# Moving the first LayerNorm's gain and offset off the router's path in a one-core decoder layer

## The chip, the cores and the metric

One core of one Trainium2 chip runs the whole layer in one launch. The metric is device time in microseconds (us). The kernel before took 1308.48 to 1312.22 us in three runs, median 1310.56 us.

## The reference, cut to what matters

256 tokens of width 1024 go through a token mixer (a Mamba-2 scan and sliding-window attention off one projection), a first LayerNorm, and a mixture of 32 experts of which each token takes four; then the second LayerNorm.

```python
m = token_mixer(x, ...)                       # 256 x 1024
h = layer_norm(alpha * x + m, ln1_g, ln1_b)   # alpha = 2 ** 0.25
logits = h @ w_router + b_router              # 1024 x 32, top 4, softmax over the four
y = layer_norm(alpha * h + moe(h), ln2_g, ln2_b)
# expert: hgu = h @ w_gate_up[e] + b; act = clamped SwiGLU; act @ w_down[e] + b_down[e]
```

All is float32. The experts' weights are 32 x (8 MB + 4 MB), read once each.

## The kernel before, in words

The order of the instructions is written out by hand, and every engine runs its own list in that order. There are three stretches.

**The front** (lines 197 to 832) multiplies x by the combined projection in slices of 256 columns. Each slice is a 1 MB load into one of two ring buffers (SP's queue, L110), is split by ACT into a rounded high part and by DVE into the remainder (L67 and L70, `split_ahead`), and costs 2 x 24 products on TensorE (PE, `mm3`). A count called `clock` goes up after each 24 products (`tick`), and side work is put on that count with `later(d, fn)`: convolution taps on DVE, the decays of the scan, attention heads. `part_dt` (L712) so sets `decays` (a small product, whose result ACT copies to `acn`) at count DD = 6 and `decay_rows` (L513, a PE transpose of `acn`, stored to DRAM) at DD + 1. The loads for the later norm and router are issued by `mix_loads` (L694) during the gate slices: x again, the rows of `ln1_g` and `ln1_b` spread over 128 partitions (512 KB each), the router's weights and bias. After the projection come the attention output product (the loop at L787, four slices), the scan's output product (L815) and the merge.

**The router stage** (L835 to L975) runs the mixing product in eight pieces `mix(c, q)` of 12 products each, for two halves c of the tokens and four weight pieces q. After a column half is complete, `resid` adds alpha * x on DVE and takes norm statistics. Then, per token half: `first_norm` (mean and reciprocal deviation by a logarithm, an exponential and a Newton step, then four DVE passes with gain and offset), `turn` (eight PE transposes of h, copied by ACT to `hT`), `logits` (eight products), `residual` (alpha * h into the four output banks by a product with `ia`), `top` (bias, top four as a mask `mk`), `place` (each token's position in its expert's list by a product with a triangular matrix) and `one_hot`. `gather(None, 0)` (L1209) then builds the inputs of experts 0 and 1 by products of h with the one-hot matrix, one ACT copy per four blocks.

**The experts** (L1215 to L1241) run a list of 384 steps ("slots"): eight steps u per expert for gate and up, four steps d for down, those of expert e - 1 after the u of expert e. A 2 MB weight tile feeds two steps. The tiles are loaded by SP (L140) into ten buffers (`NPAIR`); nine are asked for ahead, seven from expert 25 on (`st["ahead"]`); a load waits until PE has finished with the tile that held its buffer. In the router stage `prefetch(n)` issues the first ten as buffers come free. `at(n, fn, pre)` hangs further work on step n, ahead of (pre) or behind its products. Every second expert brings a gather of 16 products; every expert a transposed gate matrix S and the product `out` that adds its rows to the four output banks `po`, which stay taken from the router stage to the end. After the u steps of expert 27 all engines branch over a block for overfull experts (`overflow`, L1205), which these inputs never enter. Behind the last step the rows of `ln2_g` and `ln2_b` are loaded, spread over the partitions, and the second norm runs on DVE straight from the output banks.

Of the kernel before, what the change touches and what calls it, by code (L numbers as in the profile page):

```python
# [8 lines left out]
F = mybir.dt.float32  # L9
R = mybir.dt.float32r  # L10
I32 = mybir.dt.int32
AF = mybir.ActivationFunctionType
# [3 lines left out]
P = 128  # L16
# [6 lines left out]
NE = 32  # L23
# [21 lines left out]
def hybrid_layer(ctx, tc, x, w_in, conv_w, conv_b, dt_bias, a_log, d_skip, norm_w, w_ssm_out,  # L45
# [201 lines left out]
    for _ in range(2):  # L247
# [32 lines left out]
    io64 = const.tile([P, 2, 64], F, name="io64")  # L280
    nc.gpsimd.iota(io64, pattern=[[0, 2], [1, 64]], base=0, channel_multiplier=0,
                   allow_small_or_imprecise_dtypes=True)
# [358 lines left out]
    def rstd(dst, var, n, scale, eps, tag):  # L641

        v, y, t = [work.tile([P, n], F, name=x_ + tag, tag=x_, bufs=2) for x_ in ("rs_v", "rs_y", "rs_t")]
        ts(v, var, scale, eps, OP.mult, OP.add)
        act(y, v, AF.Ln)
        act(y, y, AF.Exp, scale=-0.5)

        def newton():
            tt(t, y, y, OP.mult)
            tt(t, t, v, OP.mult)  # L650
            ts(t, t, -0.5, 1.5, OP.mult, OP.add)
            tt(dst, y, t, OP.mult)
        return newton
# [4 lines left out]
    def gated():  # L658
# [33 lines left out]
        prefetch(1)  # L692

    def mix_loads():  # L694
        xr = single.rearrange("p (c d) -> p c d", d=D)
        nc.sync.dma_start(xr, x[0].rearrange("(c p) d -> p c d", p=P))
        lnc = [w4([P, D], n) for n in ("lng", "lnb")]
# [3 lines left out]
        nc.sync.dma_start(wr3, w_router[0].rearrange("(k p) e -> p k e", p=P))  # L701
        br = w1([P, 32], "br")
        nc.sync.dma_start(br, rows(b_router, 32))
        return xr, lnc, wr3, br

    mixin = []


# [75 lines left out]
    for i in range(2):  # L784
        nc.sync.dma_start(bgn[i], b_gate_up[0, :, D * i:D * i + D])
    mrg = gts[1]
    for n in range(4):  # L787
        hi, lo = take()
        for b in range(2):
# [48 lines left out]

    def mix(c, q):
# [5 lines left out]
        for k in range(4):  # L845
# [5 lines left out]
    xr, lnc, wr3, br = mixin  # L851
    bst = work.tile([P, 2, 2, 6], F, name="bst", bufs=1)
# [6 lines left out]
    hn = xr  # L859
    hT = [None, None]  # L860
# [4 lines left out]
    ones = const.tile([P, P], F, name="ones")  # L865
    lg, mk = (const.tile([P, 2, 32], F, name=n) for n in ("lg", "mk"))
# [3 lines left out]
    ts(ia, ident, ALPHA, None, OP.mult)  # L870
    nc.vector.memset(ones, 1.0)

# [11 lines left out]

    def norm(dst, src, bs, gb, tag):

        mean, r = norm_scale(bs, tag)()
        for hf in range(2):
            hs = slice(512 * hf, 512 * hf + 512)
            norm_half(dst[:, hs], src[hf], mean, r, gb, hs)  # L890

    def turn(c):
        hT[c] = w4([P, 8, P], f"hT{c}")
        for k4 in range(2):
            pb = bank(f"ht{c}{k4}").rearrange("p (k t) -> p k t", k=4)
            for k in range(4):
                nc.tensor.transpose(pb[:, k], hn[:, c, (4 * k4 + k) * P:(4 * k4 + k + 1) * P], ident)
            act(hT[c][:, 4 * k4:4 * k4 + 4], pb)

    pl = [None, None]  # L900

    def logits(c):
        pl[c] = bank(f"lg{c}")[:, 0:32]
        for k in range(8):
            mm(pl[c], hT[c][:, k], wr3[:, k], k == 0, k == 7)

    def top(c):
        tt(lg[:, c], pl[c], br, OP.add)
        nc.vector.max(t8[:, c], lg[:, c])
        ts(nm[:, c:c + 1], t8[:, c, 0:1], -1.0, None, OP.mult)  # L910
        nc.vector.memset(t8[:, c, 4:8], 3.0e38)
        nc.vector.match_replace(rp[:, c], t8[:, c], lg[:, c], -3.0e38)
        ts(mk[:, c], rp[:, c], -2.9e38, None, OP.is_le)

    pp = bank("pos").rearrange("p (c e) -> p c e", e=32)
    G2 = const.tile([P, 2, 2, 64], F, name="G2")

    def place(c):
        mm(pp[:, c], slt, mk[:, c], c == 0, True)
        stt(posm[:, c], pp[:, c], 1.0, mk[:, c], OP.add, OP.mult)  # L920
        ts(posm[:, c], posm[:, c], -1.0, None, OP.add)

# [8 lines left out]

    def residual(c):
        for hf in range(2):
            po[c][hf] = bank(f"out{c}{hf}")
            hs = slice(512 * hf, 512 * hf + 512)
            mm(po[c][hf], ia, hn[:, c, hs], True, False)

    def first_norm(c):
        norm(hn[:, c], [xr[:, c, 0:512], xr[:, c, 512:1024]], bst[:, c].rearrange("p a b -> p (a b)"), lnc, f"l1{c}")

# [34 lines left out]
    one_hot(0, 1)  # L975
    nxt_moe = nxt[0]
    assert nxt_moe == S_E
# [45 lines left out]
    def gather(n, j):  # L1023

        if n is not None:
            one_hot(j, 0)
            one_hot(j, 1)
        XG[j] = more.tile([P, 2, 8, 64], F, name=f"xg{j}", tag="xg")

        def unit(kq, n):  # L1030
            pb = bank(f"xg{j}{kq}").rearrange("p (q n) -> p q n", q=4)
            for k in range(4):
                o = 256 * (2 * kq + k // 2) + k % 2
                for c in range(2):
                    mm(pb[:, k], hn[:, c, o:o + 255:2], G2[:, c], c == 0, c == 1)
            ev = lambda: act(XG[j][:, :, 4 * kq:4 * kq + 4].rearrange("p e q s -> p q e s"),
                             pb.rearrange("p q (e s) -> p q e s", e=2))
# [69 lines left out]
    def done_d(n, e, b_, S):  # L1107
        y = mo.tile([P, 512], F, name="y", bufs=2)
        last = e == NE - 1

        def f():
            for c in range(2):
                for hf in range(2):
                    rs = slice(64 * hf, 64 * hf + 64)
                    mm(po[c][hf], S[rs, c * P:(c + 1) * P], y[rs], False, last)
        if last:
            act(y, b_)
            f()
        else:
            at(n + 1, lambda: act(y, b_))  # L1120
            at(n + 1, f, pre=False)


    def overflow():
        ns = (NT - cap) // 2

        def half(t, *shape):
# [11 lines left out]
        Ss = half(mo.tile([P, 512], F, name="y", bufs=2), 2, NT)  # L1139
        nc.gpsimd.iota(ios, pattern=[[ns, 2], [1, ns]], base=cap, channel_multiplier=0,  # L1140
                       allow_small_or_imprecise_dtypes=True)

        def big(w, c0, lhs, e):
            for kp in range(4):
# [3 lines left out]
                else:  # L1148
                    rows_ = w[0, e, 256 * kp:256 * (kp + 1), c0:c0 + 1024].rearrange("(k p) n -> p k n", p=P)
                nc.gpsimd.dma_start(raw, rows_)  # L1150
# [20 lines left out]
        def one_expert(e):  # L1171
            for s in range(2):
# [3 lines left out]
                for k4 in range(2):  # L1176
                    pb = bk[k4][:, 0:4 * ns].rearrange("p (k n) -> p k n", n=ns)
                    for k in range(4):
                        kk = slice((4 * k4 + k) * P, (4 * k4 + k + 1) * P)
                        for c in range(2):  # L1180
                            mm(pb[:, k], hn[:, c, kk], gs[:, 0, c], c == 0, c == 1)
                    act(xg[:, s, 4 * k4:4 * k4 + 4], pb)
                for c in range(2):
# [21 lines left out]
        with tc.If(cv > cap):  # L1205
            for e in range(NE):
                one_expert(e)

    gather(None, 0)  # L1209
    at(0, lambda: (soft(0), soft(1), nc.scalar.preload_act_table_set(SILU)), pre=False)  # L1210
# [32 lines left out]

    lnd, res = (t.rearrange("p (s d) -> p s d", d=D) for t in pair("lnd"))
    lnd = [lnd[:, 0], lnd[:, 1]]
    nc.sync.dma_start(lnd[0], rows(ln2_g, D))
    nc.sync.dma_start(lnd[1], rows(ln2_b, D))
    work = mo
# [42 lines left out]
```

## Time and profile before

| what | value |
|---|---|
| median of the runs, us | 1310.56 |
| profiled execution, us | 1311.2 |
| its span, us | 1309.4 |
| PE busy, share of span | 95% |
| PE weight loads busy | 51% |
| DVE, ACT busy | 32%, 23% |
| HBM read | 465.30 MB, 356 GB/s over the span |
| SP's queue (q1), share of 16 DMA engines | 85.7% |

The profiled execution took 1311.2 us, of which 1309.4 us are the span that the trace shows and 1.8 us lie around it. The trace names engines PE, PEld (PE's weight loads), DVE, ACT, POOL and SP. A time in a row is the start from the beginning of the span; what stands in square brackets is the idle time before an instruction on its engine, and what ended it. Matmul ends are modelled, so PE's spare time is read from bracketed idle times and from the distances between starts, not from its busy share. A float32 product is recorded as two matmuls.

### The profile page before, as it was taken

The page shows a single profiled execution, that of the slowest core. Times are in us where ns is not written, and L with a number is a line of the kernel's source. Part 1 is how long each engine was busy: PE and PEld are TensorE (multiplying, and loading weights), DVE is VectorE, ACT ScalarE, POOL GpSimd, SP SyncE. Part 2 cuts the span into 40 slices and gives each one's busy share as a digit, 9 for nine tenths or more (in the row PEclk, how much of TensorE's full clock was granted, in tenths as well). Part 3 has the DMA queues.
Part 4 walks back from the last instruction along what each step waited for, and adds up shares of the span by engine and source line. Part 5 has one row for each costly group of instructions (what it writes and reads, how often), then busy time and mean ns, then how long its engine had stood idle before and what let it go on. Part 6 is the DMA issues. An engine that isn't in the chain of part 4 may idle for free. (4 is left out here: it accounts for less than half of the span.)

```text
span 1309.4 us, 16114 instructions
## 1 busy us (share of the span) xinstructions
PE 1237.4 (95%) x6835; PEld 673.5 (51%) x6835; DVE 421.5 (32%) x813; ACT 300.0 (23%) x535; POOL 23.7 (2%) x28
## 2 busy tenths in 40 slices
PE   8899999999999999999999989899998989879995
PEld 7898878999974343343443424333333424323331
DVE  4889986665651211121111111111111111111114
ACT  3657676634411010111100101010010101000001
POOL 0001210000000000000000000000000000000000
PEclk9899999999989999999999999999999999989998
DMA  6444445776699999999999999999999999999994
GB/s 214 152 159 133 158 161 162 242 277 245 226 410 384 430 429 431 430 429 431 430 430 430 431 432 428 430 430 431 431 430 430 430 430 430 432 426 430 430 431 175
DMA packets 80003, 467.50 MB, mean 357 GB/s; under 512 B 7052, under 2 KB 46164, under 8 KB 55220
## 3 DMA queue, kind: packets, MB, share of 16 engines
q1 hardware_dynamic: 78500, 460.99, 85.7%
q0 software_dynamic: 1200, 4.33, 1.0%
q8 instruction: 55, 0.90, 0.2%
q10 hardware_dynamic: 224, 1.08, 0.2%
q14 instruction: 24, 0.20, 0.0%
HBM read 465.30 MB, written 1.08 MB: 356 GB/s over the span
## 5 line engine op out<-in xcount | busy, mean ns | idle before, releaser
L81 PE MATMUL u<-w,xg 128*64 128x512 f32 x2048 | 462.2, 597 | 19.7 <-DMA w<-in_w_gate_up_dram 19.6
L81 PEld LDWEIGHTS u<-w,xg 128*64 128x64 f32 x2048 | 140.3, 137 | 309.9 <-issue 259.3
L81 PE MATMUL d<-w,ac 128*64 128x512 f32 x1024 | 241.7, 603 | 19.1 <-DVE gg L75 9.0
L1054 DVE COPY gu<-u 128x512 f32<-128x512 f32 x32 | 22.1, 692 | 678.6 <-PE u L81 678.6
L81 PE MATMUL ws<-x,w 128*128 128x256 f32 x1200 | 156.6, 291 | 1.9 <-ACT w L67 1.8
L81 PEld LDWEIGHTS ws<-x,w 128*128 128x128 f32 x1200 | 149.8, 196 | 5.5 <-ACT w L67 2.4
L81 PEld LDWEIGHTS d<-w,ac 128*64 128x64 f32 x1024 | 68.5, 137 | 141.9 <-issue 132.8
L70 DVE TENSOR_TENSOR w<-ring,w 128x2048 fp32r<-128x2048 f32 (+1 forms) x51 | 115.4, 2268 | 38.2 <-ACT w L67 36.5
L67 ACT ACTIVATE w<-ring 128x2048 fp32r<-128x2048 f32 (+1 forms) x51 | 95.5, 1876 | 64.2 <-DMA ring<-in_w_in_dram 19.1
L67 ACT ACTIVATE gu<-u 128x512 f32<-128x512 f32 x32 | 19.1, 597 | 319.8 <-PE u L81 319.8
L81 PEld LDWEIGHTS xg<-G,single 128*128 128x128 f32 x512 | 62.9, 197 | 25.0 <-issue 24.3
L81 PE MATMUL xg<-G,single 128*128 128x128 f32 x512 | 68.9, 288 | 0.4 <-DVE G L70 0.4
L67 ACT ACTIVATE xg<-xg 128x512 f32<-128x512 f32 x32 | 19.1, 597 | 219.2 <-PE xg L81 219.2
L81 PE MATMUL out<-y,S 64*128 64x512 f32 x256 | 63.6, 615 | 0.8 <-ACT y L67 0.8
L67 ACT ACTIVATE hg<-hg 128x512 f32<-128x512 f32 x32 | 20.2, 631 | 147.8 <-DVE hg L74 147.8
L81 PE MATMUL yss<-yt,w 128*128 128x256 f32 x384 | 48.3, 289 | 0.2 <-DVE w L70 0.2
L81 PEld LDWEIGHTS yss<-yt,w 128*128 128x128 f32 x384 | 47.7, 198 | 0.6 <-DVE w L70 0.4
L81 PE MATMUL z<-w,x 128*128 128x512 f32 x192 | 47.9, 402 | 0.0
L1065 PEld LDWEIGHTS tu<-ident,gu 128*128 128x128 f32 x256 | 33.4, 210 | 25.5 <-issue 24.3
L81 PEld LDWEIGHTS out<-y,S 64*128 64x128 f32 x256 | 22.0, 186 | 41.9 <-issue 40.2
L67 ACT ACTIVATE y<-d 128x512 f32<-128x512 f32 x32 | 19.1, 597 | 105.5 <-PE d L81 105.5
L70 DVE TENSOR_TENSOR hg<-tu,bgu 128x256 f32<-128x256 f32 x64 | 26.9, 420 | 48.5 <-PE tu L1065 48.4
(214 smaller groups left out, 808.7 us busy)
## 6 DMA issues: line engine op xcount, KB each, us to landing
w<-in_w_gate_up_dram SPq DMA_DIRECT2D x128, 2048.0 KB, 38.1
w<-in_w_down_dram SPq DMA_DIRECT2D x63, 2048.0 KB, 38.7
ring<-in_w_in_dram SPq DMA_DIRECT2D x33, 1024.0 KB, 5.1
ring<-in_w_ssm_out_dram SPq DMA_DIRECT2D x8, 1024.0 KB, 5.1
E<-accd POOLq DMA_DIRECT2D x8, 512.0 KB, 4.6
ring<-in_w_attn_out_dram SPq DMA_DIRECT2D x4, 1024.0 KB, 5.2
ring<-in_w_mix_out_dram SPq DMA_DIRECT2D x4, 1024.0 KB, 7.2
single<-in_x_dram SPq DMA_DIRECT2D x2, 512.0 KB, 3.6
```

Source lines behind the costliest of these rows:

```text
L67: return nc.scalar.activation(o, i, func, **kw)
L70: return nc.vector.tensor_tensor(o, a, b, op=op)
L81: return nc.tensor.matmul(o, l, r, start=start, stop=stop)
L1054: nc.vector.tensor_copy(t, banks[hf])
L1065: nc.tensor.transpose(pb[:, b], gu[hf][:, b:b + 509:4], ident)
```

## The change

1. **Router.** The logits are formed from the residual before normalization. The gain is multiplied into the router's weights and each expert's column mean is taken off them (`router_parts`, hung on the second slice of the attention output product), so that the mean of the row drops out; the deviation is applied to the 32 logits in `top`. The offset's share goes into the bias. Transposes (`turn`) now run on the residual and are spread between the pieces of the mixing product, and `logits(0)` stands inside the last piece.
2. **Gather.** `normed` (one ACT pass) only takes off the mean and scales; gain and offset come in when the gathered rows are copied (four ACT copies in place of one). The gather of experts 0 and 1 is issued per token half.
3. **Late work.** The residual's product, and the rows of ln1 and ln2 spread over partitions by small products (`norm_rows`) from one 16 x 256 tile `lnr`, are done in steps 356 to 377 of 384, at experts 30 and 31 (and the down steps of 29 and 30).
4. **Smaller ones.** `decay_rows` two counts later; one DVE operation less in the one-column Newton step and in `place` (positions count from 1); the spread loads of the four norm vectors fall away; the never-entered overflow block follows the new gather.

```diff
+    lnr = const.tile([16, 256], F, name="lnr")
+    gbc = const.tile([P, 2, 8], F, name="gbc")
...
-        nc.sync.dma_start(lnc[0], rows(ln1_g, D))
-        nc.sync.dma_start(lnc[1], rows(ln1_b, D))
+        for i, v in enumerate((ln1_g, ln1_b, ln2_g, ln2_b)):
+            nc.sync.dma_start(lnr[4 * i:4 * i + 4], v[0].rearrange("(t n) -> t n", n=256))
...
+    def router_parts():
+        wr3 = mixin[1]
+        pb = bank("lncol")
+        for j in range(2):
+            nc.tensor.transpose(pb[:, 16 * j:16 * j + 16], lnr[:, j:j + 255:2], ident[0:16, 0:16])
+        act(gbc.rearrange("p i (t j) -> p j i t", j=2),
+            pb[:, 0:32].rearrange("p (j i t) -> p j i t", j=2, t=4)[:, :, 0:2])
...
+        def sums_():
+            tt(t, wr3, gbc[:, 1].unsqueeze(2).to_broadcast([P, 8, 32]), OP.mult)
+            nc.vector.tensor_reduce(red[:, 32:64], t.rearrange("p k e -> p e k"), op=OP.add, axis=AX.X)
+            tt(wr3, wr3, gbc[:, 0].unsqueeze(2).to_broadcast([P, 8, 32]), OP.mult)
+            nc.vector.tensor_reduce(red[:, 0:32], wr3.rearrange("p k e -> p e k"), op=OP.add, axis=AX.X)
+        def centred():
+            mm(pb[:, 64:128], ones, red, True, True)
+            stt(wr3, pb[:, None, 64:96].to_broadcast([P, 8, 32]), -1.0 / D, wr3, OP.mult, OP.add)
+            tt(br, br, pb[:, 96:128], OP.add)
+        later(1, sums_)
+        later(3, centred)
...
-        later(DD + 1, decay_rows)
+        later(DD + 3, decay_rows)
...
     for n in range(4):
         hi, lo = take()
+        if n == 1:
+            router_parts()
...
     def top(c):
-        tt(lg[:, c], pl[c], br, OP.add)
+        stt(lg[:, c], pl[c], scales[c][1], br, OP.mult, OP.add)
...
+    def normed(c):
+        mean, r = scales[c]
+        off = work.tile([P, 1], F, name="no", bufs=2)
+        stt(off, mean, -1.0, r, OP.mult, OP.mult)
+        act(xr[:, c], xr[:, c], AF.Identity, scale=r, bias=off)
...
     resid(0, 1)
+    turn(0, 0)
+    turn(1, 0)
+    first_scale(0)
     mix(1, 2)
-    first_norm(0)
-    mix(1, 3)
+    turn(0, 1)
+    scales[0] = scales[0]()
+    normed(0)
+    mix(1, 3, 0)
+    logits(0)
+    mix(1, 3, 1)
+    top(0)
     resid(1, 1)
     prefetch(10)
-    turn(0)
-    first_norm(1)
-    logits(0)
-    residual(0)
-    top(0)
-    turn(1)
     place(0)
+    turn(1, 1)
+    first_scale(1)
     one_hot(0, 0)
     logits(1)
     mm(pp[:, 1], ones, mk[:, 0], True, False)
-    residual(1)
+    scales[1] = scales[1]()
     top(1)
+    normed(1)
+    xg0 = [bank(f"xg0{kq}").rearrange("p (q n) -> p q n", q=4) for kq in range(2)]
+    first_rows(0, 0)
     place(1)
+    first_rows(0, 1)
     one_hot(0, 1)
+    first_rows(1, 0)
+    first_rows(1, 1)
...
+            def ev():
+                for k in range(4):
+                    kk = 4 * kq + k
+                    act(XG[j][:, :, kk], pb[:, k].rearrange("p (e s) -> p e s", e=2), AF.Identity,
+                        scale=gbc[:, 0, kk:kk + 1], bias=gbc[:, 1, kk:kk + 1])
...
+    def norm_rows(n, i, hf):
+        pb = bank(f"row{i}{hf}")
+        for r in range(2):
+            t = 4 * i + 2 * hf + r
+            mm(pb[:, 256 * r:256 * r + 256], ident[0:16, t:t + 1].to_broadcast([16, P]), lnr, True, True)
+        hs = slice(512 * hf, 512 * hf + 512)
+        def use():
+            if i >= 2:
+                act(lnd[i - 2][:, hs], pb)
+            else:
+                for c in range(2):
+                    tt(hn[:, c, hs], hn[:, c, hs], pb, OP.add if i else OP.mult)
+        at(n + 1, use)
+    def residual():
+        for c in range(2):
+            for hf in range(2):
+                mm(po[c][hf], ia, hn[:, c, 512 * hf:512 * hf + 512], False, False)
...
+    LATE = 8 + 12 * (NE - 3)
+    for q in range(4):
+        at(LATE + 2 * q, lambda q=q: norm_rows(LATE + 2 * q, q // 2, q % 2), pre=False)
+        at(LATE + 12 + 3 * q, lambda q=q: norm_rows(LATE + 12 + 3 * q, 2 + q // 2, q % 2), pre=False)
+    at(LATE + 10, residual, pre=False)
+    at(LATE + 11, out_tiles)
...
-    nc.sync.dma_start(lnd[0], rows(ln2_g, D))
-    nc.sync.dma_start(lnd[1], rows(ln2_b, D))
```

## Rows read from the trace of the kernel before

**Rows 1.** The page, GB/s moved in 40 equal slices of the span.
```profile
GB/s 214 152 159 133 158 161 162 242 277 245 226 410 384 430 429 431 430 429 431 430 430 430 431 432 428 430 430 431 431 430 430 430 430 430 432 426 430 430 431 175
```

**Rows 2.** Windows: stretch, length, busy time per engine, PE clock, DMA share, GB/s.
```profile
380.00:390.00 10.00, 9.57 (x44) 7.32 (x45) 1.66 (x10) 0.60 (x1) 0.50 (x1) 0.68 1.02 416
390.00:400.00 10.00, 10.00 (x53) 3.93 (x51) 1.11 (x8) 2.30 (x4) 0.00 (x0) 1.00 0.62 231
```

**Rows 3.** Timeline of SP's queue, weight tiles of the experts, router stage.
```profile
349.47 19.35 SPq L140 DMA_DIRECT2D w<-in_w_gate_up_dram  x6
...
394.58 11.34 SPq L140 DMA_DIRECT2D w<-in_w_gate_up_dram  x4
```

**Rows 4.** Timeline of PE after the expert-27 branch, up to the last expert's down steps.
```profile
1167.71 5.50 PE L81 MATMUL d<-w,ac 128*64 128x512 f32 x16 [8.63 <-DVEq L1205]
...
1264.27 3.65 PE L81 MATMUL u<-w,xg 128*64 128x512 f32 x16 [0.20 <-DMA w<-in_w_gate_up_dram]
1269.34 3.65 PE L81 MATMUL u<-w,xg 128*64 128x512 f32 x16 [1.41 <-DMA w<-in_w_gate_up_dram]
1274.28 1.94 PE L81 MATMUL d<-w,ac 128*64 128x512 f32 x8 [1.29 <-DVE gg L75]
...
1283.97 1.94 PE L81 MATMUL d<-w,ac 128*64 128x512 f32 x8 [0.77 <-DMA w<-in_w_down_dram]
```

**Rows 5.** Timeline of the front around the transpose of acn: PE, DVE, SP's queue.
```profile
53.38 0.42 PE L515 MATMUL acT<-ident,acn 128*64 128x128 f32 x1 [5.88 <-ACT acn L67]
53.45 16.95 PE L81 MATMUL ws<-x,w 128*128 128x256 f32 x120
...
57.67 6.34 SPq L110 DMA_DIRECT2D ring<-in_w_in_dram  x2
...
64.75 2.29 DVE L70 TENSOR_TENSOR w<-ring,w 128x2048 fp32r<-128x2048 f32 x1 [0.46 <-ACT w L67]
...
72.83 2.29 DVE L70 TENSOR_TENSOR w<-ring,w 128x2048 fp32r<-128x2048 f32 x1 [0.28 <-PE s L81]
```

**Rows 6.** Tile ring, loads from 20 to 120 us: issue to landing.
```profile
DMA to landing us min/median/max: 5.0/5.2/6.3
```

**Rows 7.** Windows of the front, columns as in rows 2.
```profile
50.00:60.00 10.00, 6.62 (x36) 6.63 (x37) 9.79 (x16) 5.41 (x12) 0.00 (x0) 0.66 0.55 160
150.00:160.00 10.00, 10.00 (x70) 8.94 (x69) 9.79 (x21) 9.32 (x24) 4.27 (x3) 1.00 0.33 107
290.00:300.00 10.00, 10.00 (x84) 9.82 (x82) 2.03 (x4) 2.24 (x2) 0.00 (x0) 1.00 0.83 311
```

**Rows 8.** Timeline, a small product inside the expert steps.
```profile
399.62 0.63 PE L81 MATMUL pos<-mk,ones 128*128 128x32 f32 x4
400.18 7.09 PE L81 MATMUL u<-w,xg 128*64 128x512 f32 x32
```

**Rows 9.** Timeline of PE in the router stage.
```profile
372.31 1.97 PE L81 MATMUL lg<-wr,hT 128*128 128x32 f32 x16
...
378.98 3.08 PE L81 MATMUL lg<-wr,hT 128*128 128x32 f32 x16
...
382.30 3.76 PE L81 MATMUL out<-single,ia 128*128 128x512 f32 x4
...
390.89 8.80 PE L81 MATMUL u<-w,xg 128*64 128x512 f32 x40
```

**Rows 10.** Timeline of PE around the product with the down bias.
```profile
897.95 1.94 PE L81 MATMUL d<-w,ac 128*64 128x512 f32 x8
899.82 3.69 PE L81 MATMUL out<-bd,S 32*128 32x512 f32 x8
903.45 1.94 PE L81 MATMUL d<-w,ac 128*64 128x512 f32 x8
```

**Rows 11.** Windows late in the experts, columns as in rows 2.
```profile
1182.00:1235.00 53.00, 53.00 (x260) 20.75 (x258) 8.36 (x22) 5.61 (x10) 0.00 (x0) 1.00 1.01 430
```

**Rows 12.** Lines by form: busy, mean ns | idle before, releaser.
```profile
L70 DVE TENSOR_TENSOR rs_tl<-rs_tl,rs_vl 128x1 f32<-128x1 f32 x4 | 0.6, 159 | 0.1
```

More of the change, by code (lines that the diff above doesn't have):

```diff
@@ L648, in newton @@
         def newton():
-            tt(t, y, y, OP.mult)
-            tt(t, t, v, OP.mult)
+            if n == 1:
+                stt(t, y, v, y, OP.mult, OP.mult)
+            else:
+                tt(t, y, y, OP.mult)
+                tt(t, t, v, OP.mult)
             ts(t, t, -0.5, 1.5, OP.mult, OP.add)
@@ L692, in gated @@
         prefetch(1)
+    lnr = const.tile([16, 256], F, name="lnr")
+    gbc = const.tile([P, 2, 8], F, name="gbc")
+    ones = const.tile([P, 1], F, name="ones").to_broadcast([P, P])
+    br = sm("br", 32)
     def mix_loads():
@@ L786, in hybrid_layer @@
     mrg = gts[1]
+    nc.vector.memset(ones[:, 0:1], 1.0)
     for n in range(4):
         hi, lo = take()
+        if n == 1:
+            router_parts()
         for b in range(2):
@@ L837, in hybrid_layer, with mix @@
     pm = [[bank(f"mix{c}{hf}") for hf in range(2)] for c in range(2)]
-    def mix(c, q):
+    def mix(c, q, part=None):
         hf, kh = divmod(q, 2)
@@ L844, in mix @@
         cs = slice(c * P, (c + 1) * P)
-        for k in range(4):
+        for k in range(4) if part is None else (2 * part, 2 * part + 1):
             kk = 4 * kh + k
@@ L849, in mix @@
             mm(pm[c][hf], ml[:, kk, cs], hi[:, k], False, kk == 7)
[L851 removed]
+    xr, wr3 = mixin
     bst = work.tile([P, 2, 2, 6], F, name="bst", bufs=1)
@@ L859, in hybrid_layer @@
     hn = xr
-    hT = [None, None]
+    hT = [w4([P, 8, P], f"hT{c}") for c in range(2)]
     po = [[None, None], [None, None]]
@@ L883, in norm_half, with turn @@
         stt(dst, dst, r, gb[1][:, hs], OP.mult, OP.add)
[L885 to L898, printed above, removed]
+    def turn(c, hf):
+        pb = bank(f"ht{c}{hf}").rearrange("p (k t) -> p k t", k=4)
+        for k in range(4):
+            o = 512 * hf + 256 * (k // 2) + k % 2
+            nc.tensor.transpose(pb[:, k], xr[:, c, o:o + 255:2], ident)
+        act(hT[c][:, 4 * hf:4 * hf + 4], pb)
     pl = [None, None]
@@ L913, in top, with later_top @@
         ts(mk[:, c], rp[:, c], -2.9e38, None, OP.is_le)
+    def later_top(c):
+        ts(nm[:, c:c + 1], t8[:, c, 0:1], -1.0, None, OP.mult)
     pp = bank("pos").rearrange("p (c e) -> p c e", e=32)
@@ L920, in place @@
         stt(posm[:, c], pp[:, c], 1.0, mk[:, c], OP.add, OP.mult)
-        ts(posm[:, c], posm[:, c], -1.0, None, OP.add)
     def one_hot(j, c):
@@ L930, in soft, with gathered, first_rows @@
         ts(gw[:, c], ex[:, c], sw[:, c:c + 1], None, OP.mult)
[L932 to L939, printed above, removed]
+    def normed(c):
[3 more added lines that the diff above has]
+        act(xr[:, c], xr[:, c], AF.Identity, scale=r, bias=off)
+    def gathered(c, kq, pb):
+        for k in range(4):
+            o = 256 * (2 * kq + k // 2) + k % 2
+            mm(pb[:, k], hn[:, c, o:o + 255:2], G2[:, c], c == 0 and k == 0, c == 1 and k == 3)
+    def first_rows(c, kq):
+        gathered(c, kq, xg0[kq])
     run_due()
@@ L1030, in unit @@
         def unit(kq, n):
-            pb = bank(f"xg{j}{kq}").rearrange("p (q n) -> p q n", q=4)
-            for k in range(4):
-                o = 256 * (2 * kq + k // 2) + k % 2
+            if n is None:
+                pb = xg0[kq]
+            else:
+                pb = bank(f"xg{j}{kq}").rearrange("p (q n) -> p q n", q=4)
                 for c in range(2):
-                    mm(pb[:, k], hn[:, c, o:o + 255:2], G2[:, c], c == 0, c == 1)
-            ev = lambda: act(XG[j][:, :, 4 * kq:4 * kq + 4].rearrange("p e q s -> p q e s"),
-                             pb.rearrange("p q (e s) -> p q e s", e=2))
+                    gathered(c, kq, pb)
+            def ev():
+                for k in range(4):
+                    kk = 4 * kq + k
+                    act(XG[j][:, :, kk], pb[:, k].rearrange("p (e s) -> p e s", e=2), AF.Identity,
+                        scale=gbc[:, 0, kk:kk + 1], bias=gbc[:, 1, kk:kk + 1])
             ev() if n is None else at(n + 1, ev)
@@ L1114, in f @@
                     rs = slice(64 * hf, 64 * hf + 64)
-                    mm(po[c][hf], S[rs, c * P:(c + 1) * P], y[rs], False, last)
+                    if e == 0:
+                        po[c][hf] = bank(f"out{c}{hf}")
+                    mm(po[c][hf], S[rs, c * P:(c + 1) * P], y[rs], e == 0, last)
         if last:
@@ L1178, in one_expert @@
                     for k in range(4):
-                        kk = slice((4 * k4 + k) * P, (4 * k4 + k + 1) * P)
+                        kk, o = 4 * k4 + k, 256 * (2 * k4 + k // 2) + k % 2
                         for c in range(2):
-                            mm(pb[:, k], hn[:, c, kk], gs[:, 0, c], c == 0, c == 1)
-                    act(xg[:, s, 4 * k4:4 * k4 + 4], pb)
+                            mm(pb[:, k], hn[:, c, o:o + 255:2], gs[:, 0, c], c == 0, c == 1)
+                        act(xg[:, s, kk], pb[:, k], AF.Identity, scale=gbc[:, 0, kk:kk + 1],
+                            bias=gbc[:, 1, kk:kk + 1])
                 for c in range(2):
@@ L1207, in overflow, with out_tiles @@
                 one_expert(e)
+    lnd = []
+    def norm_rows(n, i, hf):
[7 more added lines that the diff above has]
+                act(lnd[i - 2][:, hs], pb)
+            else:
+                for c in range(2):
[5 more added lines that the diff above has]
+                mm(po[c][hf], ia, hn[:, c, 512 * hf:512 * hf + 512], False, False)
+    def out_tiles():
+        a, b = (t.rearrange("p (s d) -> p s d", d=D) for t in pair("lnd"))
+        lnd.extend((a[:, 0], a[:, 1], b))
+    LATE = 8 + 12 * (NE - 3)
[4 more added lines that the diff above has]
+    at(LATE + 11, out_tiles)
     gather(None, 0)
@@ L1241, in hybrid_layer @@
             done_d(n, e, cur[0], S)
-    lnd, res = (t.rearrange("p (s d) -> p s d", d=D) for t in pair("lnd"))
-    lnd = [lnd[:, 0], lnd[:, 1]]
-    nc.sync.dma_start(lnd[0], rows(ln2_g, D))
-    nc.sync.dma_start(lnd[1], rows(ln2_b, D))
+    res = lnd[2]
     work = mo
```

23 lines of the change are left out of this document (13 added, 10 removed).

## The prediction

> **What bounds the kernel now.** I read the page's slices first. From the twelfth slice (360 us) on, the memory moves 410, 384 and then 426 to 432 GB/s, apart from the last slice [rows 1]. That is the experts' weights arriving at the most this kernel draws, 2.097 MB per tile or 4.87 us at 430; before, the rate is about half. So there are two kernels: a front up to 349 us, in which PE works nearly without a gap, and a stream of 2 MB tiles that begins when the front lets go of its buffers, the first of them at 349.47 us [rows 3]. In the stream, what counts is when it starts, whether it has holes, and what follows the last tile.
>
> Windows show one hole: 416 GB/s from 380 to 390 us and 231 from 390 to 400 [rows 2], against 430. That is (14 x 10 + 199 x 10) / 430 = 4.95 us of lost transfer. SP's queue says why: ten tiles fill the ten buffers, and the eleventh is asked for at 394.58 [rows 3], when PE has used up the first one: the experts' first product starts at 390.89, and two steps of eight records at 0.22 us (40 in 8.80 [rows 9]) end at 394.4.
>
> The end was read from PE's timeline. At expert 27 all engines meet at a branch and PE resumes at 1167.71. It then runs without idle time until 1264, and waits only four more times ahead of the last expert's down steps: 0.20, 1.41, 1.29 and 0.77 us, together 3.67 [rows 4]. The third is put down to DVE's gg, long done; it is the tile again. From 1283.97 on, PE's own work and the second norm set the end. So behind the branch PE has 3.67 us of room and no more.
>
> **The change, part by part.**
>
> *Decay rows two counts later.* PE idled 5.88 us at the transpose of acn, because ACT copies acn late [rows 5], and ran at 0.66 of full clock in the window after it [rows 7]: 120 products took 16.95 us [rows 5], against 14.3 where 84 of this width fill 10 us at full clock [rows 7]. Stall and slow clock together: 5.9 + 2.6 = 8.5 us. Two counts on (48 products, 5.7 us) acn is there. But DVE and the ring are late next. DVE was busy through the stall, 9.79 of 10 us [rows 7]. Its split at 64.75 waits (0.46 us) for a slice whose load leaves at 57.67 [rows 5], when an earlier split has freed that half of the ring, and takes 5.0 to 6.3 us to land [rows 6]; DVE did nothing else before, so this stays. The next split, at 72.83, hangs on the second of these loads, which leaves at 57.67 + 6.34 - 0.37 = 63.64 [rows 5]: landing at 68.7, ACT's half 1.9, hence 70.6 instead of 72.83: 2.2 us won. DVE is still 98% busy at 150 to 160 us [rows 7], so PE, ahead of it, waits for it there. I take -2.2; bounds -8.5 (all kept) and 0.
>
> *Router parts.* Two transposes and one small product enter a PE list that has no gap there. Two such products take 0.56 us of list [rows 8]; I take +0.7 (0.3 to 1.5). ACT's copy and DVE's six operations on 256 elements are hidden: DVE is busy 2.03 of 10 us in that stage [rows 7]. Without that cover they would be 2.4 us. SP issues four tiny loads in place of two of 512 KB, which costs it under 1 us in a stretch where it waits for buffers; nothing.
>
> *Router stage.* Off the path fall four DVE passes per token half and two pairs of residual products, the second of which took 3.76 us with the clock at its lower level, 1.2 GHz [rows 9]. The list becomes, with durations of before: mix pieces end 3.7 us later (three turns of 0.6, logits 1.97 [rows 9]), at 374.9. Tiles eight and nine are therefore asked for at 375 and not 371; six tiles from 350 on keep the stream fed to 379, so this costs nothing; without that cover it would be the 3.7. Then on the path: residual half 0.7, turn and its copy 1.3, logits 2.0, top 1.1, shift and ACT pass of `normed(1)` 1.3, eight products of the gather 1.9: experts start near 383.5, 7.4 earlier. If the clock falls as it did from 379 on (logits 3.08 instead of 1.97 [rows 9]), near 386.5. The ACT copies at the gather's end (four for one) lie beside the other half's products. The eleventh tile would then be asked for at 387 to 390, just before the stream runs dry at 391.5. So the hole closes: at most -4.95 [rows 2]; with the slow clock about -2.4; I take -4.3. Nothing further is won: the rest of the 7.4 us only makes PE wait for tiles later.
>
> *Steps 356 to 377.* These are the steps of experts 30 and 31, and PE reaches step 356 at 1230, behind the branch. Added: 16 products of 16 x 256 columns and 4 of 512 columns. The nearest row is the down bias's product, 32 partitions x 512 columns: four of them hold the list from 899.82 to 903.45, 3.63 us, and the step before takes 1.87 [rows 10] where eight records more add 1.71 (3.65 - 1.94 [rows 4]): 0.16 for the joint. At 0.91 per product, a quarter of the partitions is no cheaper than all of them (3.76 for two at half the clock [rows 9], 0.94 at full). So the residual costs 3.8. A norm unit has a quarter of these columns, 0.91, and the joint on either side, 1.2; eight make 9.6, less some 0.2 each in three steps where other work stands already: 9.0. Of 12.8, 3.67 fill the waits, which leaves 9.1; I take +9.0; bounds 0 (all hidden) and +10. DVE's eight passes and ACT's four copies lie in steps where both wait for PE. The stream is not slowed: seven tiles ahead are 34 us.
>
> *Second norm.* Its chain loses one DVE operation of 159 ns per half [rows 12] and its hand-over: -0.35. The spread loads of the last norm rows stood in SP's queue behind the last tile and were used after the last product, so their loss gives nothing.
>
> Sum: -2.2 + 0.7 - 4.3 + 9.0 - 0.35 = +2.85 us. On the profiled execution, 1311.2, that is 1314.05. The median of the runs stands 0.64 lower, at 1310.56, and so I put the median after at **1313.4**.
>
> The Trainium skill, "Perfetto Trace Analysis", section "Identifying the Most-Contended Engine", says that a matmul's busy share is a bad measure of PE's distance from its limit and that the busy share of weight loads is a better one. Here weight loads are busy 20.75 of 53 us from 1182 to 1235 while the matmul row shows 53.00 [rows 11]. By that rule PE would have room for the late work, and the sum would be without the 9.0. That the same row's 260 records stand one after another without idle speaks against it.
>
> **Rivals.**
> *The late work is hidden.* PE has more room than the four waits show, and the 12.8 us go into it. Then the term of 9.0 falls away: 1313.4 - 9.0 = 1304.4. For it: the ends of matmuls are modelled. The rule above speaks for it as well. Against: steps at 1182 to 1235 follow each other at a fixed distance, and PE does wait, visibly, when a tile is late [rows 4].
> *The front keeps all of the 8.5 us.* If DVE catches up faster than I read: 1313.4 - 6.3 = 1307.1. For it: a ring load needs only 5 us where PE needs 5.7 for its slice. Against: DVE at 98% a hundred microseconds later [rows 7].
> *The hole stays open, and the kernel is slower.* The second half's path is a chain of hand-overs between PE, DVE and ACT, `normed(1)` stands behind `top(1)` on DVE, and the last gather products wait for both. If the clock falls earlier and stays low, experts start at 390 again; from a start of 388 on each microsecond is lost from the 4.3. With all of it lost: 1317.7. For it: clock of 0.68 from 380 to 390 [rows 2] after as many short products. Against: the residual's products are gone from this very stretch.
>
> **How the numbers follow.** A measurement tells changes of 0.3% (3.9 us) from none, so faster is below 1306.6 and slower above 1314.5. The forecast's case has 0.60, its own range 1310 to 1317 by the bounds of its terms; hidden late work 0.18; front kept 0.08; hole open 0.14. Faster: 0.15 of the hidden case, 0.03 of the kept front, 0.03 of the forecast's edge: 0.21. Slower: 0.11 of the open hole and 0.21 of the forecast's case: 0.32. The rest, 0.47, is within. The range reaches from 1305.0, into the hidden case, to 1317.8, the open hole.
>
> **What would show each step.** In the front: no idle time at the transpose of acn, new PE waits for DVE between 80 and 165 us, and the mixing product starting about 1.5 us earlier. In the router stage: first u product 5 to 8 us earlier relative to the first mix product, and no window under 400 GB/s. Late: norm units of about 1.2 us each in PE's list, no wait for a tile behind the branch, and the last expert's down steps running some 9 us later relative to PE's resumption than 116.3 (1283.97 - 1167.71 [rows 4]). Wrong would be: waits for tiles still there at expert 31, or the distance from resumption to the last down steps unchanged.

## The result, and the profile after

| | kernel before | changed kernel |
|---|---|---|
| median of 4 runs each | 1310.24 us (1308.48 to 1312.22) | 1320.65 us (1318.68 to 1322.50) |
| ratio of the runs | 1 | 1.0079, 95% interval 1.0057 to 1.0101 |
| profiled execution, its span | 1311.2, 1309.4 us | 1319.58, 1317.8 us |

The kernel became 10.4 us slower, outside the range that reached to 1317.8. Three moments of each profile split the difference: the load with which the stream of tiles starts (the front's end), PE's return from the branch at expert 27, and the last product into `out`, with which PE ends. That load is called the first tile here; in the list of tiles it is the third, since two leave already in the front, at 279.80 and 312.43 us in the kernel before.

| | first tile | branch left | last product | from tile to branch | from branch to last product |
|---|---|---|---|---|---|
| before | 349.47 | 1167.71 | 1294.40 | 818.24 | 126.69 |
| after | 347.32 | 1166.97 | 1303.09 | 819.65 | 136.12 |
| difference | -2.15 | -0.74 | +8.69 | +1.41 | +9.43 |

The last column was forecast: +9.0. The column before it was not: the closed hole should have brought the branch 4.3 us nearer to the first tile, and it lies 1.4 us farther off. So the first question is where some 5.7 us between 350 and 1167 us went. The page's slices of the changed kernel, GB/s, to be laid against [rows 1]:

```profile
GB/s 207 156 158 159 142 149 159 230 290 228 261 418 429 428 427 427 427 428 428 428 426 428 428 427 426 428 428 427 428 429 428 427 428 427 427 424 427 426 406 52
```

The hole in the thirteenth slice (384 before) is gone: 429. But the slices behind it show mostly 427 or 428, where [rows 1] have mostly 430 or 431. A loss of 0.7% in each slice escapes the eye, and over 815 us it is 5.7 us. Three windows of the changed kernel (columns as in [rows 2]) say the same; the first two cover the former hole, the third is the one of [rows 11]:

```profile
380.00:390.00 10.00, 10.00 (x49) 3.64 (x50) 1.42 (x10) 4.08 (x10) 0.00 (x0) 1.00 1.00 396
390.00:400.00 10.00, 10.00 (x51) 3.94 (x48) 3.39 (x11) 1.23 (x2) 0.00 (x0) 1.00 1.02 431
1182.00:1235.00 53.00, 53.00 (x260) 21.11 (x258) 9.64 (x24) 7.44 (x16) 0.00 (x0) 1.00 1.01 427
```

So 396 and 431 stand where 416 and 231 stood [rows 2], and the clock column is 1.00 where it was 0.68. The 396 is under the 400 that the prediction had named as a sign, but it is worth only (428 - 396) x 10 / 428 = 0.75 us. From 1182 to 1235 us the DMA engines are as busy as before (1.01) and move less, 427 against 430 GB/s, so they do not wait for work: each transfer takes longer. The DMA view of 700 to 1100 us, packets by size, shows that they are the same transfers, first of the kernel before:

```profile
DMA packets 11818, 172.18 MB, mean 430 GB/s; under 512 B 1308, under 2 KB 1308, under 8 KB 1308
```

and of the changed kernel:

```profile
DMA packets 11745, 171.05 MB, mean 428 GB/s; under 512 B 1304, under 2 KB 1304, under 8 KB 1304
```

172.18 MB in 11818 - 1308 large packets is 16,384 bytes each, one buffer's row of one partition; 171.05 MB in 10441 is the same. Only 0.7% fewer arrive.

The other steps are in the changed kernel's timelines. SP's queue, to be laid against [rows 3]: the eleventh tile of the list leaves 36.6 us after the first of the stream instead of 45.1.

```profile
347.32 20.36 SPq L140 DMA_DIRECT2D w<-in_w_gate_up_dram  x6
...
383.95 11.34 SPq L140 DMA_DIRECT2D w<-in_w_gate_up_dram  x4
```

PE's timeline at the transpose of acn, against [rows 5], where it waited 5.88 us, and at the experts' first product, against [rows 9]:

```profile
54.55 0.30 PE L515 MATMUL acT<-ident,acn 128*64 128x128 f32 x1 [0.30 <-ACT acn L67]
...
380.26 8.80 PE L81 MATMUL u<-w,xg 128*64 128x512 f32 x40
```

And PE's timeline behind the branch, against [rows 4]; `row` is a norm unit, `out<-single,ia` the residual:

```profile
1166.97 6.53 PE L81 MATMUL d<-w,ac 128*64 128x512 f32 x16 [8.58 <-DVEq L1263]
...
1235.53 3.65 PE L81 MATMUL u<-w,xg 128*64 128x512 f32 x16
1239.12 1.12 PE L81 MATMUL row<-lnr,ident 16*128 16x256 f32 x4
1240.17 3.65 PE L81 MATMUL u<-w,xg 128*64 128x512 f32 x16
...
1258.30 3.70 PE L81 MATMUL out<-single,ia 128*128 128x512 f32 x8
1261.93 1.94 PE L81 MATMUL d<-w,ac 128*64 128x512 f32 x8
...
1303.09 1.99 PE L81 MATMUL out<-y,S 64*128 64x512 f32 x8 [0.76 <-ACT y L67]
```

A unit holds the list 1.05 us (1239.12 to 1240.17), the residual 3.63, and nowhere from 1170 us to the last product stands a wait for a tile: the 3.67 us of [rows 4] are filled.

### The profile page after: what moved, and what is told of

It is laid out like the page before. It is cut to its first block, busy times and chain, and to the rows that moved or that the text cites. A ratio compares the mean times of both kernels' runs of the same rounds, so it can differ in the third digit from the quotient of the medians.

```text
span 1317.8 us, 16302 instructions
## 1 busy us (share of the span) xinstructions
PE 1244.7 (94%) x6871; PEld 674.1 (51%) x6871; DVE 422.4 (32%) x815; ACT 333.9 (25%) x638; POOL 23.7 (2%) x28
## 5 line engine op out<-in xcount | busy, mean ns | idle before, releaser
L81 PE MATMUL u<-w,xg 128*64 128x512 f32 x2048 | 463.4, 597 | 22.2 <-DMA w<-in_w_gate_up_dram 22.1
L1109 DVE COPY gu<-u 128x512 f32<-128x512 f32 x32 | 22.1, 692 | 671.4 <-PE u L81 671.4
L67 ACT ACTIVATE w<-ring 128x2048 fp32r<-128x2048 f32 (+1 forms) x51 | 95.5, 1877 | 67.8 <-DMA ring<-in_w_in_dram 23.2
L67 ACT ACTIVATE xg<-xg,gbc 128x128 f32<-128x128 f32 x128 | 48.1, 458 | 198.0 <-PE xg L81 198.0
```

Of the source, the lines that this page charges most:

```text
L67: return nc.scalar.activation(o, i, func, **kw)
L81: return nc.tensor.matmul(o, l, r, start=start, stop=stop)
L1109: nc.vector.tensor_copy(t, banks[hf])
```

## The experiments

**Why the transfers got slower.** Addresses are no part of a profile. The first column below was read from the compiled programs; the distances between its rows also follow from the edits, with each tile rounded up to 32 bytes. In the kernel before, the ten 16 KB tile buffers lie behind 6784 bytes of constants in each partition; the change alters these constants (`lnr` and `gbc` are new, `ones` shrinks from 512 bytes to 4) and so moves all ten buffers by 608 bytes:

```
kernel           first buffer at   past a multiple of 256
before               23296                  0
after                23904                 96
a_even               23936                128
b_odd                23328                 32
a_256                23808                  0
b_128                23424                128
b_512                23552                  0
a_512_early          24064                  0
```

That was the first theory; the rival was the changed kernel's own traffic, above all ACT's copies of the gathered rows, 128 of 458 ns. All times below were taken in turn with the kernel before on the same chip, in three sessions, in which the kernel before had medians of 1311.28, 1311.89 and 1311.21 us; each ratio is to the kernel before of the same session.

*a_even.*

```diff
-    ones = const.tile([P, 1], F, name="ones").to_broadcast([P, P])
+    ones = const.tile([P, 16], F, name="ones")[:, 0:1].to_broadcast([P, P])
```

> The changed kernel with one small constant (the column of ones) taking 64 bytes of each partition instead of 4, so that the ten tile buffers and all that lies behind them start 32 bytes further on, at a multiple of 64 bytes as in the kernel before; nothing else differs. Theory A (the address of the tile buffers slows the stream): the stretches from 440 us on go from 427 to 428 GB/s back to 430 to 431, PE comes out of the branch some 5.5 us earlier (1161 to 1162 instead of 1166.97 us), and the time falls from 1320.65 to about 1315 us. Theory B (the scaled gather copies on ACT, 128 of 458 ns, or other traffic of the changed kernel slow the stream): 427 to 428 GB/s and 1320 to 1321 us, as before the edit. Theory C (the chip of that day was slower): the kernel before would itself show it, and this one stays at 427 to 428.

Measured: 1320.76 us, ratio 1.0066 (1.0049 to 1.0084), 428 GB/s from 700 to 1100 us. A miss for theory A as it was put: a start at a multiple of 64 is not enough.

*b_odd.*

```diff
     io64 = const.tile([P, 2, 64], F, name="io64")
+    const.tile([P, 8], F, name="spare")
```

> The kernel before with 32 unused bytes among its constants, so that the ten tile buffers start 32 bytes past a multiple of 64, as they do in the changed kernel; nothing else differs. Theory A: the stream falls from 430 or 431 to 427 or 428 GB/s, PE comes out of the branch some 5 us later (1173 instead of 1167.71 us), and the time rises from 1310.2 to about 1315.5 us. Theory B: 430 GB/s and 1310 us, nothing changes.

Measured: 1321.55 us, ratio 1.0072 (1.0057 to 1.0087), 427 GB/s (in a profile of its slowest run, 1326.42 us). That is 6 us more than theory A had said. Thirty-two bytes that nothing reads or writes make the kernel before as slow as the changed one. So the address does count, and a_even had picked the wrong multiple. Both results hold together if 128 bytes past a multiple of 256 is as bad as 32.

*a_256* takes three small constants from ahead of the buffers to behind them; only the buffers and what lies between move.

```diff
     gran = ctx.enter_context(tc.tile_pool(name="gran", bufs=NPAIR))
+    tail = ctx.enter_context(tc.tile_pool(name="tail", bufs=1))
...
-    ones = const.tile([P, 1], F, name="ones").to_broadcast([P, P])
+    ones = tail.tile([P, 1], F, name="ones").to_broadcast([P, P])
...
-    cnt = const.tile([1, 1], F, name="cnt")
-    cnti = const.tile([1, 1], I32, name="cnti")
+    cnt = tail.tile([1, 1], F, name="cnt")
+    cnti = tail.tile([1, 1], I32, name="cnti")
```

> The changed kernel with three of its small constants (96 bytes of each partition) put behind the ten tile buffers instead of ahead of them: the buffers alone start 96 bytes earlier, at a multiple of 256 bytes as in the kernel before, and all else that is written or read in the experts lies where it lay in the changed kernel. Theory A, narrowed by a_even (a multiple of 64 or 128 bytes is not enough, 256 is): the stream goes from 427 to 428 back to 430 to 431 GB/s, PE leaves the branch some 5.5 us earlier, and the time is about 1315 us. Theory B (the address decides nothing for the changed kernel; its own traffic holds the stream at 427 to 428): 1320.7 us and 427 to 428 GB/s, as a_even.

Measured: 1311.84 us, ratio 1.001 (0.9999 to 1.0021), 8.8 us under the changed kernel. Its slices, and its packets from 700 to 1100 us (line numbers of this kernel and of those made from it are one higher):

```profile
GB/s 218 152 155 160 146 147 160 231 295 228 262 422 431 431 431 429 431 431 429 430 430 432 431 429 430 431 431 431 431 429 431 431 430 431 429 427 429 432 413 54
```

```profile
DMA packets 11819, 172.14 MB, mean 430 GB/s; under 512 B 1311, under 2 KB 1311, under 8 KB 1311
```

Both are those of the kernel before, with all of ACT's copies still there: the rival falls. The time fell by 3 us more than expected. From tile to branch it is 813.66 us (1158.26 - 344.60) against 819.65, 6.0 us; the first tile also leaves 2.7 us earlier. More profiles bear that out: with the changed front it leaves at 347.3 to 349.1 us in the three with buffers off a multiple of 256 and at 343.5 to 346.9 in the five on one, 2.9 us earlier on average. The front's loads go into buffers of the same pool, and the page's row of ACT's half of the split shows how long it waits for them. First the changed kernel, then a_256 (busy, mean ns | idle before, and what ended most of it):

```profile
L67 ACT ACTIVATE w<-ring 128x2048 fp32r<-128x2048 f32 (+1 forms) x51 | 95.5, 1877 | 67.8 <-DMA ring<-in_w_in_dram 23.2
```

```profile
L68 ACT ACTIVATE w<-ring 128x2048 fp32r<-128x2048 f32 (+1 forms) x51 | 95.4, 1878 | 62.5 <-DMA ring<-in_w_in_dram 19.4
```

ACT's work is the same, its waits for the ring are 23.2 against 19.4 us. Over the same eight profiles the averages are 22.4 and 19.9 us, with ranges that touch (21.3 to 23.2 and 18.1 to 21.6), so that the front's loss has this as its likely cause, which is not shown.

A third reading would be that PE reads the moved tiles more slowly and so holds their buffers longer. The pages' rows of the products for gate and up speak against it: a product takes 597 ns on average in the changed kernel and in a_256, and PE waits longer for these tiles with the slower stream, 22.1 against 19.4 us.

*b_128* and, of the third session, *b_512* are b_odd with 128 and 256 spare bytes:

```diff
-    const.tile([P, 8], F, name="spare")
+    const.tile([P, 32], F, name="spare")
...
-    const.tile([P, 8], F, name="spare")
+    const.tile([P, 64], F, name="spare")
```

> The kernel before with 128 unused bytes among its constants, so that the tile buffers start at a multiple of 128 bytes that is no multiple of 256. Theory A, narrowed: 427 to 428 GB/s as in a_even and b_odd, and some 5 to 10 us more than the kernel before, 1316 to 1321 us. Theory B (only a start that is no multiple of 64 slows the stream, and a_even was slow for a reason of its own): 430 GB/s and 1310 to 1311 us.

> The kernel before with 256 unused bytes among its constants: the tile buffers start at a multiple of 512 bytes, where they started at a multiple of 256 only. Theory A (a multiple of 256 is what counts, and a shift as such costs nothing): 430 to 431 GB/s from 440 us on and 1310 to 1312 us, as the kernel before. Rival 1 (the finer the multiple the faster): over 432 GB/s and under 1307 us. Rival 2 (any move of the buffers costs, whatever the multiple): 427 to 428 GB/s and 1318 us or more.

Measured: b_128 1319.84 us, ratio 1.0066 (1.0052 to 1.0081), 427 GB/s; b_512 1311.32 us, ratio 1.0001 (0.9991 to 1.0011), 430 GB/s. To move the buffers by 256 bytes costs nothing, by 128 it costs 8 us, and 512 wins nothing over 256. *a_512_early* repeats that on a_256_early, a faster version told of below:

```diff
-    br = sm("br", 32)
+    br = const.tile([P, 32], F, name="br")
...
-    dtv, av, nega = sm("dtv"), sm("av"), sm("nega", 32)
+    dtv, av, nega = sm("dtv"), sm("av"), const.tile([P, 32], F, name="nega")
```

> a_256_early with two small tiles of the front (128 bytes each) moved among the constants, so that the buffers start at a multiple of 512 bytes. Theory A: 430 to 431 GB/s and 1303 to 1304 us, as a_256_early. Rival 1: over 432 GB/s and under 1300 us.

Measured: 1302.96 us, ratio 0.9942 (0.9926 to 0.9959), 430 GB/s, as a_256_early. Theory A as a_256 narrowed it stands: starts 32, 96 and 128 bytes past a multiple of 256 all give 427 or 428 GB/s, four starts at a multiple give 430 or 431.

The Trainium skill states such a border in "DMA: Bandwidth & Descriptors", section "How a descriptor splits into AXI transactions": a descriptor is cut into transactions of 256 bytes that must begin at a multiple of 256, and one which starts elsewhere begins with a partly used transaction from the multiple below. On the border the runs agree with it. But it tells this of bytes that are read, and here it is the written side that starts off the border; that both are one mechanism is not shown. On the size the runs do not agree: by its count a row of 16,384 bytes would be 65 transactions instead of 64, 1.6% by my estimate, and counted in its beats of 32 bytes (513, 515 and 516 for 512, again an estimate) the loss would rise with the distance from the border, from 0.2 to 0.8%; measured is 0.7%, the same at 32, 96 and 128 bytes.

**Whether the late work sets the end.** *a_even_dma2* and *a_256_dma2* bring the second norm's rows by transfers behind the last tile, as the kernel before does, on a_even and on a_256:

```diff
-        at(LATE + 12 + 3 * q, lambda q=q: norm_rows(LATE + 12 + 3 * q, 2 + q // 2, q % 2), pre=False)
-    at(LATE + 11, out_tiles)
...
+    out_tiles()
     res = lnd[2]
+    nc.sync.dma_start(lnd[0], rows(ln2_g, D))
+    nc.sync.dma_start(lnd[1], rows(ln2_b, D))
```

> As a_even, and the second norm's gain and offset rows come by two broadcast transfers after the last tile, as in the kernel before; the four late products with their copies that replaced them are gone. Theory (late work on PE sets the end): four times about 1.2 us go from PE behind the branch, and the time is 4 to 5 us under a_even, about 1310.5 us. Rival (tiles would be waited for instead): waits for tiles behind the branch come back, up to the 3.7 us that the kernel before shows there, and the gain is under 2 us, about 1313 to 1314.

> a_256 and a_even_dma2 together: buffers at a multiple of 256 bytes, and the second norm's rows by two transfers at the end. If both theories hold, 5.5 us for the stream and 5 us for the late products add up: about 1310 us. Rival: with both, PE catches up with the tiles behind the branch and waits for them, so that the two together give 1.5 to 3 us less than their sum, 1312 to 1313 us.

Measured: a_even_dma2 1315.55 us, 5.2 under a_even; a_256_dma2 1307.54 us, ratio 0.9968 (0.9956 to 0.9980), 4.3 under a_256. The four units of 1.05 us come back whole on either base, and the two effects add up: 8.8 + 5.2 = 14.0 us expected under the changed kernel, 13.1 measured. No wait for a tile returned.

*a_256_early* also takes the rest of the late work away from the end. Each quarter of the residual is scaled into a spare tile in the middle of the experts:

```diff
-        at(LATE + 2 * q, lambda q=q: norm_rows(LATE + 2 * q, q // 2, q % 2), pre=False)
-    at(LATE + 10, residual, pre=False)
+        at(8 + 12 * (13 + 2 * q) + 1, lambda q=q: residual(8 + 12 * (13 + 2 * q) + 1, q), pre=False)
...
+            for c in range(2):
+                tt(y3[:, c], hn[:, c, 256 * q:256 * q + 256], rw[:, 0], OP.mult)
+                tt(y3[:, c], y3[:, c], rw[:, 1], OP.add)
...
+            for c in range(2):
+                mm(po[c][q // 2][:, 256 * (q % 2):256 * (q % 2) + 256], ia, y3[:, c], False, False)
```

> a_256_dma2, and the residual product with the first norm's rows taken from the steps behind the branch to the middle of the experts, where the rows show PE waiting for tiles: at the experts 14, 16, 18 and 20 one quarter each, scaled by gain and offset into a spare tile of 128x512 so that the gathers' source is left as it is. Nothing of the change's late work is left behind the branch. Theory (late work on PE sets the end, and ahead of the branch PE has 2 to 9 us to spare per 100 us): another 8.7 us of PE go from behind the branch, less up to 3.7 us of waits for tiles that come back: 1301 to 1305 us. Rival (PE has no such room, and the branch comes later by what is put there): about 1310 us, as a_256_dma2.

Measured: 1303.49 us, ratio 0.9942 (0.9928 to 0.9956): 4.1 under a_256_dma2 and 7.6 under the kernel before (0.58%). Its PE timeline at expert 14 shows the price there, and then what happens behind the branch:

```profile
750.60 1.12 PE L82 MATMUL row<-lnr,ident 16*128 16x256 f32 x4
751.65 3.65 PE L82 MATMUL u<-w,xg 128*64 128x512 f32 x16
755.24 1.13 PE L82 MATMUL out<-y,ia 128*128 128x256 f32 x4
756.30 7.09 PE L82 MATMUL u<-w,xg 128*64 128x512 f32 x32
764.30 1.94 PE L82 MATMUL d<-w,ac 128*64 128x512 f32 x8 [0.92 <-DMA w<-in_w_down_dram]
...
1259.39 3.65 PE L82 MATMUL u<-w,xg 128*64 128x512 f32 x16 [1.35 <-DMA w<-in_w_gate_up_dram]
1264.32 1.94 PE L82 MATMUL d<-w,ac 128*64 128x512 f32 x8 [1.28 <-DVE gg L76]
1274.04 1.94 PE L82 MATMUL d<-w,ac 128*64 128x512 f32 x8 [0.80 <-DMA w<-in_w_down_dram]
```

Eight microseconds after the 2.1 us of additional work PE waits for a tile again, so the work was free; the branch comes no later (813.88 us behind the first tile, 813.66 in a_256). Behind the branch the tile waits of [rows 4] are back, 3.4 us, and with them the distance to the last product is that of the kernel before: 127.11 us. The late work cost 4.3 + 4.1 = 8.4 us in all.

**The front.** *b_decay3* is the kernel before with this one line of the change, *a_256_early_d1* is a_256_early without it (the same line the other way round):

```diff
-        later(DD + 1, decay_rows)
+        later(DD + 3, decay_rows)
```

> The kernel before with one part of the change: decay_rows two counts later. If the front's gain is kept: the first prefetched tile is issued at about 347.4 us instead of 349.47, the PE clock does not fall around 55 us, and the time is about 2.1 us lower, 1308.1 us. Rival (the hole in the stream at 380 to 400 us, or the branch, takes it back): the tile starts earlier and the time stays within 0.7 us of 1310.2.

> a_256_early with decay_rows put back to one count after decays, as in the kernel before: the first part of the change undone alone. If its 2.2 us are real and kept: the wait of 5 to 6 us ahead of acT and the half-speed clock behind it are back around 55 us, the first prefetched tile is issued 1.5 to 2.5 us later, and the time is about 2 us longer, 1305 to 1306 us. Rival (the front's gain is lost ahead of the stream): 1303.5 us, no difference.

Measured: b_decay3 1309.67 us, 1.6 under the kernel before, ratio 0.9978 (0.9965 to 0.9991); its first tile leaves at 348.11 us. a_256_early_d1 1305.53 us, 2.0 above a_256_early, ratio 0.9962 (0.9946 to 0.9977) against 0.9942. The two intervals overlap, but the two runs of the same session that differ from it by this line and nothing else that counted, a_256_hole and a_512_early, have medians of 1303.58 and 1302.96 us, 2.0 and 2.6 lower. In a_256_early_d1 the first tile leaves at 348.05, and the stall is back:

```profile
53.71 0.42 PE L516 MATMUL acT<-ident,acn 128*64 128x128 f32 x1 [6.03 <-ACT acn L68]
```

Taken alone and undone alone, the gain of this line is 1.6 and 2.0 us, and it reaches the end.

**A hole put back: a miss.** *a_256_hole* was meant to test the price of the hole by itself:

```diff
-    st["ahead"] = AH
+    st["ahead"] = 6
...
+    at(8, lambda: st.update(ahead=AH))
     gather(None, 0)
```

> a_256_early with a hole put back into the stream: the prefetch runs 6 tiles ahead until the first step of the fifth tile and 9 from there on, so that the eleventh to thirteenth tiles are issued 14 us later, at about 395 us, when the tenth has long landed (about 386 us). Nothing else differs, and PE has tiles in stock until 425 us. Theory (the stream sets when PE reaches the branch, so a hole costs its whole length): 8 to 9.5 us without transfers between 385 and 397 us, the branch as much later than 1157.4 us, and 1311 to 1313 us. Rival (PE, busy without a break from 390 to 700 us, is the bound there and covers the hole): 1303 to 1305 us.

Measured: 1303.58 us, ratio 0.9942 (0.9927 to 0.9956). Neither theory was tested, since the edit made no hole:

```profile
346.21 20.33 SPq L141 DMA_DIRECT2D w<-in_w_gate_up_dram  x6
...
382.79 11.34 SPq L141 DMA_DIRECT2D w<-in_w_gate_up_dram  x4
```

The eleventh tile of the list leaves 36.58 us after the first of the stream, as in a_256_early (380.07 - 343.48 = 36.59). SP runs through its own list, and here what holds the load is its buffer coming free: naming it six tiles ahead instead of nine moved nothing. The run serves as a repeat of a_256_early.

## Why the prediction was wrong

The step that failed is a sentence, "The stream is not slowed: seven tiles ahead are 34 us", and with it a term that the sum did not have. I asked whether late work could starve the stream, and not whether the same transfers would still take the same time. The diff shows new constants ahead of the pool of tile buffers; I read them as operands and not as bytes that push the buffers 608 bytes on, off a multiple of 256. That term measures +8.8 us (1320.65 to 1311.84; 9.0 by the two ratios), of which the profiles put 6.0 between first tile and branch and 2.7 in the front. Without that term the change stands at 1.001 (0.9999 to 1.0021) of the kernel before, +1.3 us, where the sum said +2.85. Why a start off a multiple of 256 costs just this much stays open. The terms one by one, at buffers on a multiple of 256:

- *Decay rows, -2.2:* right, -1.6 and -2.0. The stall of 5.88 us went to 0.30, and waits for DVE took part of its place, as argued (3.0 us of new ones from 80 to 165 us, and 0.8 ahead of that). The rival that the front keeps 8.5 us is out. That the first tile left 2.15 us earlier in the first pair of profiles was luck: the slower loads are in it. On buffers at a multiple of 256 the changed front ends 3.7 us earlier on average than in the kernel before and b_512 (349.47 and 348.86), and what lies beyond the decay rows in this is not explained (the five spread over 3.4 us).
- *Router parts, +0.7:* not resolved. The first tile leaves at 343.5 to 346.9 us in five profiles of such fronts, and that spread hides it. Its sign is open too: a_256_early_d1, whose front has all of the change but the decay rows, lets the tile go at 348.05, no later than the kernel before.
- *Hole, -4.3:* from first tile to branch it is 813.3 to 814.4 us in six profiles with the new router stage and 817.4 to 818.2 in three with the old one, 3.9 less on average (813.83 against 817.68). The traces show what became of it: in the first 90 us of the stream 37.37 to 37.45 MB arrive in the six and 35.50 to 35.61 in the three, 1.85 MB more on average, which is 4.3 us at 430 GB/s. The experts' first product comes 32.9 us after the first tile (380.26 - 347.32) instead of 41.4, and the clock did not fall. The rival of the open hole is out: it came nearest in time, at 1317.7, and the slices show no hole. No run isolates the hole: the one that should have done so did not.
- *Late work, +9.0:* right, 8.4 us by the two runs that take it away. The unit was 1.05 us and not 1.2. The rival of hidden late work is out: the work cost its full length less the waits for tiles. With it falls, for this stretch, the rule of the Trainium skill ("Perfetto Trace Analysis", section "Identifying the Most-Contended Engine") that the prediction set beside this rival. It had promised room, with weight loads busy for 21.11 of 53 us.
- *Second norm, -0.35:* from the last product to the span's end it is 14.7 us instead of 15.0.

The range missed for the same reason: none of its cases held a price on all transfers at once. Its forecast's case also ended too low: the upper bounds that its terms state, 0, +1.5, -2.4, +10 and -0.35, reach 1319.3 and not 1317, which is still under the 1320.65 measured.

## What to carry to other kernels

Read an edit to the tiles of a pool as a move of everything placed behind it: list the start addresses of the transfer targets in both programs, and keep them at a multiple of 256 bytes where the stream of transfers is the bound, as here. When the whole of a stream is 0.5 to 1% slower with the same packets and the same busy share, look at addresses before traffic. And put small work where the bound engine waits for another: the residual with the first norm's rows cost 4.1 us behind the branch, where they left no wait for a tile, and nothing measurable in the middle of the experts.

## What the runs showed of the hardware that was not expected

The start of a buffer in its partition changes what a full stream draws: 430 to 431 GB/s at a multiple of 256 bytes, 427 to 428 at 32, 96 or 128 bytes past one, with 16 KB packets in both cases. The front ends some 2.9 us later with it, for which slower loads of 1 MB are the likely cause. A start at a multiple of 128 that is none of 256 is as slow as one at 32, and 512 is no faster than 256. No run starts 64 bytes past.
